# Two sums for the first norm, a new order of the third block pair, exchanged bank groups: one change in three places of a two-layer hybrid transformer kernel

## The chip, the cores and the metric

The kernel runs on one core of a Trainium2 chip. What is measured is the device time of one execution in microseconds (us). A profile is one further execution, taken by the hardware profiler.

## The reference, cut to what matters

Two layers work on 256 latent tokens and 256 context tokens of 1024 channels, all in float32. Each layer is a feed-forward block, a mixer (a short convolution in layer 0, grouped-query attention in layer 1) and a second feed-forward block. Each of the six norms is modulated by a vector that comes from the conditioning inputs:

```python
def _rms(t, g):
    y = t32 * lax.rsqrt(jnp.mean(t32 * t32, axis=-1, keepdims=True) + NORM_EPS)
    return y.astype(t.dtype) * g
def _modulate(t, g, shift, scale):
    return _rms(t, g) * (1 + scale) + shift
def _swiglu(h, w13, w2):
    gte, up = jnp.split(h @ w13, 2, axis=-1)
    return (jax.nn.silu(gte) * up) @ w2
...
mod = (jax.nn.silu(c) @ mod_w[i] + mod_b[i])          # 9 x 1024 per layer
lat = lat + 0.5 * mod[:, 0, 2] * _swiglu(_modulate(lat, norm_g[i, 0], mod[:, 0, 0], mod[:, 0, 1]), ...)
...                                                    # mixer, then a second _swiglu
y = ob.swapaxes(0, 1).reshape(bsz, t, D_MODEL) @ w_o   # attention, output projection
```

## The kernel before, in words

**Layout.** The state `x` lies with channels on the 128 partitions: eight blocks of 128 channels (k = 0 to 7), each 512 tokens wide (256 latent, 256 context). Every matrix product of two float32 operands is made of three TensorE products, because both operands are split into a high part (`hh`, `wh`; written by ScalarE) and a low part (`hl`, `wl`; written by VectorE as the rest): high by high, high by low, low by high. A helper `mm3` (lines 146 to 148) issues the three. Inside the first block the helper `part_of(i, k, n)` (line 1318) issues one of the three, n = 0 for `hh` by `wh`, 1 for `hh` by `wl`, 2 for `hl` by `wh`, for both halves `pg` and `pu` of output tile i: two TensorE instructions each time. `product(i, k)` is n = 0, 1, 2 for one k, `products(i, q)` is `product` for the block pair k = 2q, 2q + 1.

**The opening, written out by hand.** Inside `with tc.manual_schedule(engines=set(QUEUES))` the four queues TensorE, VectorE, ScalarE and SyncE issue in the order of the program text. The first block computes, while the weights still arrive, the mean of squares of every token, the modulation of the first norm and the first three output tiles (i = 0, 1, 2) of the first feed-forward product. Its steps are:

- `fill(idle, WARM)` (line 1080): 14 products of ones, which nobody reads, two TensorE instructions each.
- `spread_c` (line 1272): 16 steps that copy the activated conditioning over all partitions with a product by the identity `ident` (a part of the constants `cst`), two instructions each; `keep_c` (line 1278) moves the result out of the four `cs` banks.
- `square(k, ...)` writes the squares of block k (k = 0, 1 by VectorE, line 1149; the others by ScalarE, line 1151, k = 7 in two halves). `pair_sum(j)` (line 1155) adds two of them on VectorE, which leaves four partial sums; `token_sums(ps, k)` (line 1159) sums one over the partitions with 8 TensorE instructions, so 32 for the four.
- the root and reciprocal, `tile_rows` and `tile_turn` (lines 1171 and 1183; the modulation of one block by TensorE), the row products `rb` (line 1374), the normed block `over_tile` (line 1199), and `high_part` and `low_part` (lines 1290, 1298, 1303), which apply scale and shift and split into `hh` and `hl`.
- for the later blocks `mod_pe` and `mod_turn` (lines 1211 and 1233, then VectorE lines 1238 and 1245) give scale and shift of several blocks at once. Those of block 7 come from `end_units` (line 165, two units of VectorE for the scale and two for the shift), which read the tiles `mt`. `w_hi` and `w_lo` (lines 1135 and 1139) split the weights of the three output tiles in three pieces; `over_rms(q, ris)` (line 1283) norms a block pair; `norm_k` and `norm_q` are the high and low parts of one block or of a pair.

The end of the block is, before the change: three `products(i, 2)` for blocks 4 and 5 output tile by output tile, then block 6 for all three output tiles, then block 7 for all three.

**After it** the order is the planner's: outside of such blocks it orders the instructions by its own costs and by when operands come ready. There follow the gates of the three output tiles (`w13_post`: line 698 on ScalarE, line 700 on VectorE, the split at lines 122 and 123), the fourth and fifth output tile (`load_w` splits their weights at lines 122 and 123 into two halves of tags `wh`, `wl`, four buffers each, which the weights of the first two output tiles held; products at lines 146 to 148), and `FirstBlocks.sums` (lines 399 to 406), which builds sums of blocks for the rest of the product.

**The banks.** The accumulators lie in eight PSUM banks. `use_banks` opens groups of them in the order given, the first group on the lowest banks, and reuse is released tile by tile (`reuse_waits="tile"`). During attention the groups are `ptp` (banks 0, 1), `psc` (banks 2 to 5, tiles of two banks) and `pav` (banks 6, 7). The last `psc` tile is `py2`, the first two output tiles (m = 0, 1) of the output projection; it lies on banks 2 and 3. The projection's loop then reads it and exchanges the groups:

```python
    for m in range(KT):
        if m < 2:
            ps = py2[:, m, :]
        else:
            w = wo(m)
            ps = psum("py")
            for k in range(KT):
                mm3(ps[:, :S], w(k), aos[k], k == 0, k == KT - 1)
        gated(m, ps[:, :S], gate)          # VectorE, line 2007
        if m == 1:
            use_banks(("pss", 2), ("psm", 6))
```

`psum` takes the next of the six `psm` banks in turn, so m = 2 gets bank 2 before the change. The weights of m = 2, 3 are split at lines 1702 (ScalarE) and 1705 (VectorE).

Of the kernel before, what the change touches and what calls it, by code (L numbers as in the profile page):

```python
# [15 lines left out]
ALU = mybir.AluOpType  # L16
# [5 lines left out]
S = 256  # L22
T2 = 2 * S
# [6 lines left out]
EPS = 1e-6  # L30
FIRST = 5
PER_PAIR = 0.7
WARM = 14
HALVED = 2, 8
CUTS = (0, 256), (256, 512), (512, 1024)
CONSTS = (
# [12 lines left out]
def hybrid_kernel(ctx: ExitStack, tc: tile.TileContext, a: dict, out: bass.AP):  # L49
    nc = tc.nc  # L50
# [9 lines left out]
    def use_banks(*pools):  # L60
        stage.close()
        for name, bufs in pools:
            banks[name] = stage.enter_context(
                tc.tile_pool(
                    name=name, bufs=bufs, space=bass.MemoryType.PSUM, reuse_waits="tile"
                )
            )
# [351 lines left out]
    class Border:  # L419
# [38 lines left out]
        def square(self, i, s):  # L458
            sq = self.sq[i, s] = tp.tile([P, S], F32, name=nm("sq"), tag="t", bufs=3)
            nc.scalar.activation(out=sq, in_=x[:, 6 + i, s * S : s * S + S], func=AF.Square)  # L460
            self.scaled(6 + i, s)
# [615 lines left out]
    def fill(ps, n):  # L1077

        for _ in range(n):
            nc.tensor.matmul(ps[:, :P], square_ones, square_ones, start=True, stop=True)  # L1080
# [69 lines left out]
        else:  # L1150
            nc.scalar.activation(out=dst, in_=src, func=AF.Square)

    def pair_sum(j, c0=0, c1=T2):
        t = sqs[2 * j][:, c0:c1]
        nc.vector.tensor_tensor(out=t, in0=t, in1=sqs[2 * j + 1][:, c0:c1], op=ALU.add)

    def token_sums(ps, k):
        for i in range(4):
            nc.tensor.matmul(
                ps[:, i : i + 1], sqs[k][:, i * P : i * P + P], ones,  # L1160
                start=k == 0 and i == 0, stop=k == KT - 2, skip_group_check=True,
            )
# [92 lines left out]
    def end_units(ch):  # L1255
        for v in range(2):
            mod_unit(0, ch, KT - 1, end_raw[ch], v)
        if ch:
            nc.vector.scalar_tensor_tensor(
                out=A00[:, KT - 1, :], in0=modv[0, 1][:, KT - 1, :], scalar=1.0,  # L1260
                in1=normg[:, 0, 0, KT - 1 :].to_broadcast([P, 2]), op0=ALU.add, op1=ALU.mult,
            )
# [3 lines left out]
    def spread_c(i, n=1):  # L1266


        for i in range(i, i + n):
            v, k = i // KT, i % KT  # L1270
            o = k % 4 * P
            nc.tensor.matmul(
                spread[i // 4][:, o : o + P], sccol[:, k, v : v + 1].to_broadcast([P, P]), ident,
                start=True, stop=True,
            )
# [30 lines left out]
    def norm_k(k):  # L1306
        for s in range(2):
            high_part(k, s)
            low_part(k, s)

    def norm_q(q):
        for k in (2 * q, 2 * q + 1):
            norm_k(k)
# [10 lines left out]
    def product(i, k):  # L1324
        for n in range(3):
            part_of(i, k, n)

    def products(i, q):
        for k in (2 * q, 2 * q + 1):
            product(i, k)  # L1330
# [7 lines left out]
    with tc.manual_schedule(engines=set(QUEUES)):  # L1338
        for k in range(2):
            for ch in (1, 0):  # L1340
                ask_tile(ch, k)
            ask_w(k, 0)
        ask_w(2, 0)
        for ch in (1, 0):
            ask_mod(ch, 1)
        for i in range(2):
            ask_w(i, 1)
        table(AF.Silu)
        nc.scalar.activation(out=sccol[:, :, :2], in_=ccol, func=AF.Silu)
        table(AF.Sqrt)  # L1350
        for i in range(4):
            spread[i] = psum("cs")
        ps = psum("ss")
        fill(idle, WARM)
        spread_c(0, 6)
        for k, eng in enumerate((nc.vector, nc.vector) + (nc.scalar,) * 5):
            square(k, eng)
            if k % 2:
                pair_sum(k // 2)
                token_sums(ps, k - 1)  # L1360
                spread_c(6 + k // 2)
        for s in range(2):
            square(7, nc.scalar, s * S, s * S + S)
            pair_sum(3, s * S, s * S + S)
        token_sums(ps, 6)
        for i in range(2):
            keep_c(i)
        rs = tp.tile([P, 4], F32, name="rs4", tag="rs4", bufs=1)
        nc.scalar.activation(out=rs, in_=ps[:, :4], func=AF.Sqrt, scale=1.0 / D, bias=eps_t)
        nc.vector.reciprocal(rs, rs)  # L1370
        tile_rows(0)
        rb = psum("rb")
        for i in range(4):
            nc.tensor.matmul(
                rb[:, i * P : i * P + P], rs[:, i : i + 1].to_broadcast([P, P]), ident,
                start=True, stop=True,
            )
        nc.vector.tensor_scalar(
            out=sb1, in0=modb[:, 0, KT : 2 * KT], scalar1=1.0, scalar2=None, op0=ALU.add
        )  # L1380
        w_hi(0, 0)
        over_tile(0, 0, rb)
        tile_turn(0)
        over_tile(0, 1, rb)
        pps[0] = psum("pg"), psum("pu")
        spread_c(9, 7)
        for s in range(2):
            high_part(0, s)
        for i in range(2, 4):
            keep_c(i)  # L1390
        pps[1] = psum("pg"), psum("pu")
        w_lo(0, 0)
        for s in range(2):
            low_part(0, s)
        for s in range(2):
            part_of(0, 0, 0, s * S, s * S + S)
        part_of(0, 0, 1)
        tile_rows(1)
        for ch in (1, 0):
            ask_mod(ch, 2)  # L1400
        w_hi(1, 0)
        w_lo(1, 0)
        ris = tp.tile([P, T2], F32, name="ris", tag="gm", bufs=3)
        nc.scalar.copy(ris, rb)
        w_hi(2, 0)
        for s in range(2):
            over_tile(1, s, ris)
        part_of(0, 0, 2)
        part_of(1, 0, 0)
        tile_turn(1)  # L1410
        for n in (1, 2):
            part_of(1, 0, n)
        pps[2] = psum("pg"), psum("pu")
        part_of(2, 0, 0)
        w_lo(2, 0)
        for s in range(2):
            high_part(1, s)
            low_part(1, s)
        for n in (1, 2):
            part_of(2, 0, n)  # L1420
        product(0, 1)
        over_rms(1, ris)
        table(AF.Silu)
        mod_pe(1, 1)
        mod_pe(0, 1)
        for ch in (1, 0):
            ask_tile(ch, 2)
        ask_w(2, 1)
        for i, ch in enumerate((1, 0)):
            ask_end(ch)  # L1430
            ask_w(i, 2)
        ask_w(2, 2)
        product(1, 1)
        w_hi(0, 1)
        w_lo(0, 1)
        mod_turn(1, 1)
        mod_turn(0, 1)
        w_hi(1, 1)
        norm_q(1)
        product(2, 1)  # L1440
        products(0, 1)
        w_hi(2, 1)
        w_lo(1, 1)
        over_rms(2, ris)
        w_lo(2, 1)
        mod_pe(1, 2)
        mod_pe(0, 2)
        end_units(1)
        products(1, 1)
        w_hi(0, 2)  # L1450
        mod_turn(1, 2)
        mod_turn(0, 2)
        w_lo(0, 2)
        norm_q(2)
        products(2, 1)
        w_hi(1, 2)
        w_lo(1, 2)
        over_rms(3, ris)
        products(0, 2)
        w_hi(2, 2)  # L1460
        w_lo(2, 2)
        products(1, 2)
        norm_k(6)
        end_units(0)
        products(2, 2)
        for i in range(3):
            product(i, 6)
        norm_k(7)
        for i in range(3):
            product(i, 7)  # L1470
        for ch in HALVED:
            b = modb[:, :, ch * KT : ch * KT + KT]
            nc.vector.tensor_scalar(out=b, in0=b, scalar1=0.5, scalar2=None, op0=ALU.mult)
# [551 lines left out]
    for m in range(KT):  # L2025
        if m == KT - 2:
            ready()
# [6 lines that stand above are left out]
                mm3(ps[:, :S], w(k), aos[k], k == 0, k == KT - 1)  # L2034
        gated(m, ps[:, :S], gate)
        if m == 1:
            use_banks(("pss", 2), ("psm", 6))
        square_add(m, 0, S)
        hi, lo = xa(m, 0), xa(m, 1)
        nc.scalar.activation(out=hi[:, :S], in_=x[:, m, :S], func=AF.Identity, scale=A[:, m, :1])  # L2040
        nc.vector.scalar_tensor_tensor(
            out=lo[:, :S], in0=x[:, m, :S], scalar=A[:, m, :1], in1=hi[:, :S].bitcast(F32),
            op0=ALU.mult, op1=ALU.subtract,
        )
        for part, t in enumerate((hi, lo)):
            nc.scalar.copy(
                t[:, S:], bs[:, part, m : m + 1].bitcast(F32).to_broadcast([P, 2])
            )
# [260 lines left out]
```

## Time and profile before

| | |
|---|---|
| runs before | 1554.48 us median of 3 (1553.35 to 1557.8) |
| the profiled execution | 1553.15 us, of which the span of the instructions is 1551.4 us |
| granted TensorE clock, mean | 1.000 |
| TensorE busy | 1544.8 us of the span |
| VectorE busy | 1308.3 us |
| ScalarE busy | 763.7 us |
| data moved | 247.72 MB, 160 GB/s mean |

A row of the timeline gives the start in us from the start of the span, how long the row lasts in us, engine, line and operation, the written tile and the read ones (`out<-in`), the form, how many instructions are merged into the row (x28), and in brackets how long the engine was idle before it and what ended that. A TensorE row ends later than the next one starts, because products are pipelined: what one costs is the distance of the starts. A row of the windows gives for each engine the busy time and, in brackets, the number of instructions. DVE is VectorE, ACT ScalarE, PE TensorE, PEld its weight loads, SP SyncE.

### The profile page before, as it was taken

What the parts mean: (1) busy time and instruction counts of PE and PEld (TensorE: products, weight loads), DVE (VectorE), ACT (ScalarE), POOL (GpSimd) and SP (SyncE); (2) the same over time, 40 slices, a digit from 0 to 9 for tenths busy, and PEclk for the clock granted to TensorE, in tenths of its full rate; (3) what the DMA queues carried; (4) which work ended last, traced back from release to release, by engine and by line L of the source; (5) the groups of instructions that cost most, each with busy time, mean ns of one, the idle gap of its engine ahead of it and who ended that gap; (6) DMA issues with size and microseconds to landing.
All of it is one profiled execution on the core that took longest, in us unless ns stands there. A gap on an engine that the chain in (4) does not pass through costs nothing.

```text
span 1551.4 us, 25405 instructions
## 1 busy us (share of the span) xinstructions
PE 1544.8 (100%) x10296; PEld 1419.6 (92%) x10296; DVE 1308.3 (84%) x1944; ACT 763.7 (49%) x1285; POOL 28.9 (2%) x24
## 2 busy tenths in 40 slices
PE   9999999999999999999999999999999999999999
PEld 7899899989888899988999899988999899998888
DVE  5988889997999689987998989987998877878653
ACT  5554245536322475522554475522554465776551
POOL 0000000000000000000000000000000002220000
PEclk9999999999999999999999999999999999999999
DMA  9433633354565423355333632356344743346551
GB/s 358 136 109 129 211 123 123 121 201 167 178 221 195 140 86 119 114 178 197 123 129 124 218 120 105 114 189 227 136 142 165 264 146 120 109 171 244 190 176 70
DMA packets 52005, 247.72 MB, mean 160 GB/s; under 512 B 6064, under 2 KB 9264, under 8 KB 36656
## 3 DMA queue, kind: packets, MB, share of 16 engines
q1 hardware_dynamic: 51600, 245.91, 46.2%
q8 instruction: 80, 1.31, 0.3%
q14 instruction: 37, 0.30, 0.1%
q10 hardware_dynamic: 288, 0.19, 0.0%
HBM read 243.72 MB, written 1.05 MB: 158 GB/s over the span
## 4 chain that ended last, share of the span: by engine, by line
PE 99%; ACT 0%; DVE 0%; issue 0%; ACTq 0%
PE py L146 9%; PE py L148 9%; PE py L147 9%; PE p L146 7%; PE p L148 7%; PE p L147 7%; PE q L148 5%; PE q L146 5%; PE q L147 5%; PE py L1994 3%; PE pu L1994 3%; PE pg L1994 3%; PE pv L146 1%; PE pv L148 1%; PE pg L545 1%; PE pv L147 1%
## 5 line engine op out<-in xcount | busy, mean ns | idle before, releaser
L165 DVE CUSTOM_DVE_ANT_0 junk<-wm,scbc,cst 128x1024 bf16<-128x1024 f32 x224 | 287.2, 1282 | 32.3 <-DMA wm<-in_modT 30.6
L122 ACT ACTIVATE wh<-wr 128x1024 fp32r<-128x1024 f32 (+1 forms) x196 | 178.0, 925 | 215.8 <-PE py L147 124.9
L123 DVE TENSOR_TENSOR wl<-wr,wh 128x1024 fp32r<-128x1024 f32 (+1 forms) x196 | 205.8, 1060 | 51.5 <-PE py L1994 22.9
L146 PE MATMUL py<-gh,wh 128*128 128x512 f32 (+1 forms) x594 | 217.8, 367 | 0.0
L147 PE MATMUL py<-gl,wh 128*128 128x512 f32 (+1 forms) x594 | 217.3, 366 | 0.0
L148 PE MATMUL py<-gh,wl 128*128 128x512 f32 (+1 forms) x594 | 217.1, 365 | 0.0
L773 ACT ACTIVATE wh<-wr 128x1024 fp32r<-128x1024 f32 x165 | 169.5, 1056 | 86.1 <-DVE wr L796 65.5
L776 DVE TENSOR_TENSOR wl<-wr,wh 128x1024 fp32r<-128x1024 f32 x165 | 196.8, 1218 | 15.4 <-ACT wh L773 15.3
L148 PEld LDWEIGHTS py<-gh,wl 128*128 128x128 f32 x594 | 112.0, 189 | 17.9
L146 PEld LDWEIGHTS py<-gh,wh 128*128 128x128 f32 x594 | 112.1, 189 | 17.5
L147 PEld LDWEIGHTS py<-gl,wh 128*128 128x128 f32 x594 | 112.1, 189 | 17.4
L148 PE MATMUL p<-th,wl 128*128 128x256 f32 x440 | 124.5, 283 | 0.0
L147 PE MATMUL p<-tl,wh 128*128 128x256 f32 x440 | 124.5, 283 | 0.0
L146 PE MATMUL p<-th,wh 128*128 128x256 f32 x440 | 124.5, 283 | 0.0
L146 PE MATMUL q<-bh,wh 128*128 128x256 f32 x304 | 86.0, 283 | 0.0
L147 PE MATMUL q<-bl,wh 128*128 128x256 f32 x304 | 86.0, 283 | 0.0
L148 PE MATMUL q<-bh,wl 128*128 128x256 f32 x304 | 86.0, 283 | 0.0
L146 PEld LDWEIGHTS p<-th,wh 128*128 128x128 f32 x440 | 84.5, 192 | 0.2
L147 PEld LDWEIGHTS p<-tl,wh 128*128 128x128 f32 x440 | 84.5, 192 | 0.2
L148 PEld LDWEIGHTS p<-th,wl 128*128 128x128 f32 x440 | 84.5, 192 | 0.0
L791 DVE TENSOR_TENSOR wr<-wr 128x1024 f32<-128x1024 f32 x55 | 67.4, 1225 | 1.8
L148 PE MATMUL q<-th,wl 128*128 128x256 f32 x220 | 62.9, 286 | 0.0
(394 smaller groups left out, 4101.0 us busy)
## 6 DMA issues: line engine op xcount, KB each, us to landing
wr<-in_w SPq DMA_DIRECT2D x85, 1024.0 KB, 4.9
wm<-in_modT SPq DMA_DIRECT2D x128, 512.0 KB, 4.2
wr<-in_w2h SPq DMA_DIRECT2D x48, 704.0 KB, 4.4
wr<-in_cw_cx SPq DMA_DIRECT2D x8, 1024.0 KB, 5.6
wr<-in_w2l SPq DMA_DIRECT2D x8, 1024.0 KB, 4.9
mr<-in_mod SPq DMA_DIRECT2D x8, 512.0 KB, 8.6
wr<-in_cw_b SPq DMA_DIRECT2D x4, 1024.0 KB, 5.5
wr<-in_cw_out SPq DMA_DIRECT2D x4, 1024.0 KB, 5.2
```

Of the source, the lines that this page charges most:

```text
L122: nc.scalar.activation(out=hi, in_=src, func=AF.Copy)
L123: nc.vector.tensor_tensor(out=lo, in0=src, in1=hi.bitcast(F32), op=ALU.subtract)
L146: nc.tensor.matmul(ps, wh, mh, start=first, stop=False, **kw)
L147: nc.tensor.matmul(ps, wh, ml, start=False, stop=False, **kw)
L148: nc.tensor.matmul(ps, wl, mh, start=False, stop=last, **kw)
L165: nc.vector.tensor_tensor_reduce(out=junk, in0=raw, in1=scbc[:, v, :], scale=0.5 if ch in HALVED else 1.0, scalar=modb[:, l, col : col + 1 ...
L545: nc.tensor.matmul(ps, w[n == 1], hl if n == 2 else hh, start=first and n == 0 and k == ks[0] and (first is True or g == 0), stop=last and ...
L773: nc.scalar.activation(out=self.shaped(g, 0), in_=self.part(g), func=AF.Copy)
L776: nc.vector.tensor_tensor(out=self.shaped(g, 1), in0=self.part(g), in1=self.shaped(g, 0).bitcast(F32), op=ALU.subtract,)
L791: tt(out=by_two(raw[:, :1024]), in0=a21.unsqueeze(1).to_broadcast([P, 2, T2]), in1=by_two(raw)[:, :, :T2], op=ALU.subtract,)
L1994: nc.tensor.matmul(p[:, :n], w(j, k)[part], m(k)[:, :n], start=not part and k == 0, stop=part == 1 and k == nk - 1, skip_group_check=True,)
```

## The change

Three places are edited. In the opening, 11 and not 14 fills come first, all 16 steps of `spread_c` come at once instead of 6, then one behind each of three token sums, then 7 later, five more fills follow them, VectorE adds the squares of blocks 0 to 5 to one sum and those of 6 and 7 to another, and TensorE takes two `token_sums` instead of four; in the later place of the seven `spread_c` there are six fills. In the third block pair, the shift units of block 7 (`end_units(0)`) move up to directly behind its scale units, blocks 4 and 5 are multiplied in an order written out by part, blocks 6 and 7 are normed together, and their products run output tile by output tile. At the output projection the two bank groups are opened in the other order, so that `psm` starts at bank 0.

```diff
-WARM = 14
+WARM = 11
+FILL = 6
...
-    def pair_sum(j, c0=0, c1=T2):
-        t = sqs[2 * j][:, c0:c1]
-        nc.vector.tensor_tensor(out=t, in0=t, in1=sqs[2 * j + 1][:, c0:c1], op=ALU.add)
+    def add_square(i, k, c0=0, c1=T2):
+        t = sqs[i][:, c0:c1]
+        nc.vector.tensor_tensor(out=t, in0=t, in1=sqs[k][:, c0:c1], op=ALU.add)
...
         fill(idle, WARM)
-        spread_c(0, 6)
-        for k, eng in enumerate((nc.vector, nc.vector) + (nc.scalar,) * 5):
-            square(k, eng)
-            if k % 2:
-                pair_sum(k // 2)
-                token_sums(ps, k - 1)
-                spread_c(6 + k // 2)
-        for s in range(2):
-            square(7, nc.scalar, s * S, s * S + S)
-            pair_sum(3, s * S, s * S + S)
+        spread_c(0, 16)
+        fill(idle, 5)
+        for k in range(6):
+            square(k, nc.vector if k < 2 else nc.scalar)
+            if k:
+                add_square(0, k)
+        square(6, nc.scalar)
+        for c in (0, S):
+            square(7, nc.scalar, c, c + S)
+            add_square(6, 7, c, c + S)
+        token_sums(ps, 0)
         token_sums(ps, 6)
         for i in range(2):
             keep_c(i)
...
         over_tile(0, 1, rb)
         pps[0] = psum("pg"), psum("pu")
-        spread_c(9, 7)
+        fill(pps[0][0], FILL)
         for s in range(2):
             high_part(0, s)
...
         mod_pe(1, 2)
         mod_pe(0, 2)
         end_units(1)
+        end_units(0)
         products(1, 1)
         w_hi(0, 2)
         mod_turn(1, 2)
         mod_turn(0, 2)
         w_lo(0, 2)
         norm_q(2)
         products(2, 1)
         w_hi(1, 2)
         w_lo(1, 2)
         over_rms(3, ris)
-        products(0, 2)
         w_hi(2, 2)
         w_lo(2, 2)
-        products(1, 2)
-        norm_k(6)
-        end_units(0)
-        products(2, 2)
+        for i, k, n in (
+            (0, 4, 0), (0, 5, 0), (0, 4, 1), (0, 4, 2), (0, 5, 1),
+            (1, 4, 0), (1, 5, 0), (0, 5, 2), (1, 4, 2), (1, 5, 2), (1, 4, 1), (1, 5, 1),
+            (2, 4, 0), (2, 5, 0), (2, 4, 2), (2, 5, 2), (2, 4, 1), (2, 5, 1),
+        ):
+            part_of(i, k, n)
+        norm_q(3)
         for i in range(3):
-            product(i, 6)
-        norm_k(7)
-        for i in range(3):
-            product(i, 7)
+            products(i, 3)
...
         if m == 1:
-            use_banks(("pss", 2), ("psm", 6))
+            use_banks(("psm", 6), ("pss", 2))
```

## The prediction

> **What bounds the kernel now.** I read the page first (busy times, then the chain that ended last), then TensorE's waits, then the timeline of the places that the change touches.
>
> ```profile
> PE 1544.8 (100%) x10296; PEld 1419.6 (92%) x10296; DVE 1308.3 (84%) x1944; ACT 763.7 (49%) x1285; POOL 28.9 (2%) x24
> ...
> PE 99%; ACT 0%; DVE 0%; issue 0%; ACTq 0%
> ```
>
> ```profile
> PE py L146 <- DVE x L2007: 1.3, 1, 1.3
> PE idle L1080 <- DVE eps_t L105: 1.1, 1, 1.1
> PE pg L146 <- ACT wh L122: 0.7, 1, 0.7
> ```
>
> TensorE is busy throughout, its own instructions make 99% of the chain, and it has three waits in the whole run: the start, one of 0.7 us ahead of the fourth output tile's `pg`, one of 1.3 us in the output projection. So work taken from VectorE or ScalarE is worth nothing unless it ends one of these waits, and the whole change can gain little more than the two waits plus whatever it takes from TensorE's own list. What it can lose is larger: every stall that a new order makes on TensorE is added in full.
>
> **Part one, the opening.** Here TensorE's timeline, then the landing of the constants, then ScalarE and VectorE beside it.
>
> ```profile
> 1.07 6.29 PE L1080 MATMUL idle<-sones 128*128 128x128 f32 x28 [1.07 <-DVE eps_t L105]
> 7.19 1.50 PE L1272 MATMUL cs<-cst,sccol 128*128 128x128 f32 x12
> 8.53 0.95 PE L1159 MATMUL ss<-ones,sq 128*128 128x1 f32 x8
> 9.34 0.47 PE L1272 MATMUL cs<-cst,sccol 128*128 128x128 f32 x2
> ...
> 11.88 0.95 PE L1159 MATMUL ss<-ones,sq 128*128 128x1 f32 x8
> ...
> 17.02 0.28 PE L1318 MATMUL pg<-hh,wh 128*128 128x256 f32 x1
> ```
>
> ```profile
> L89 ACTq DMA_DIRECT2D cst<-in_cst x1: 450/450/450, 1.2 to 1.2; - x1
> ...
> DMA to landing us min/median/max: 5.4/5.4/5.4
> ```
>
> ```profile
> 6.52 2.29 ACT L1151 ACTIVATE sq<-x 128x512 f32<-128x512 f32 x4
> ...
> 15.76 1.09 ACT L1290 ACTIVATE hh<-hr,mod,A 128x256 fp32r<-128x256 f32 x2 [0.86 <-DVE mod L1191]
> ```
>
> ```profile
> 7.69 0.69 DVE L1155 TENSOR_TENSOR sq<-sq,sq 128x512 f32<-128x512 f32 x1 [1.01 <-ACT sq L1151]
> ...
> 10.01 0.76 DVE L1155 TENSOR_TENSOR sq<-sq,sq 128x256 f32<-128x256 f32 x2 [0.47 <-ACT sq L1151]
> ```
>
> The two more additions of VectorE cost nothing: the five go into one sum, the last four behind ScalarE's squares, which are ready from about 7.1 on (four in 2.29 us from 6.52). Four times 0.69 from 7.1 ends at 9.9, before the last pair at 10.01, which ends at 10.77 as before. TensorE reads that sum after 11.88 already now, so the cover is over 1 us, and the additions would cost only what they overran it.
>
> Nor do the sums bind TensorE, so only its own list counts. Ahead of `tile_rows` it held 28 instructions of fills, 18 of spreading and 32 of token sums, 78 in all; now it holds 22, 32, 10 more fills and 16 token sums, 80. Sixteen instructions go and eighteen come. But the rows show two paces: the 28 fills take 6.12 us (1.07 to 7.19), 0.219 each, the 12 of the spreading take 1.34 us (7.19 to 8.53), 0.112 each, in the same shape. The slow pace is that of the first 6 us, not of an instruction. In that time the kernel before does 28 instructions. The new list has only 22 that can run: the 23rd reads the constants, which land at 1.16 + 5.4 = 6.6 (the row prints the start as 1.2). 22 fills end at 1.07 + 22 x 0.219 = 5.9, so TensorE stands for 0.7 us, does 2.7 instructions until 7.19, the other 29.3 of the spreading at 0.112 until 10.5, ten fills until 11.6, and two token sums of 0.81 us each (8.53 to 9.34) until 13.2. Before, the fourth ends at 11.88 + 0.81 = 12.7. That is 0.5 us later, and all the rest of the chain (root, reciprocal, row products, high parts) hangs on it.
>
> Later, 12 instructions of fills stand in for 14 of spreading, at most 2 x 0.112 = 0.22 us less. The second high part ends at 15.76 + 1.09 = 16.85 and TensorE takes it at 17.02, so of the 0.22 only about 0.1 can be used before that high part is what is late. The opening costs 0.4 us. Its bounds: -0.1, if the constants arrive before 5.9 (then the token sums end at 12.8, and the 0.22 may count in full), and +3.2, if the pause prolongs the slow pace (rival one).
>
> **Part two, the third block pair.** TensorE first, then VectorE, then ScalarE.
>
> ```profile
> 43.41 0.39 PE L1318 MATMUL pg<-hh,wh 128*128 128x512 f32 x1
> ...
> 59.51 0.39 PE L1318 MATMUL pu<-hl,wh 128*128 128x512 f32 x1
> 60.59 0.50 PE L146 MATMUL pg<-hh,wh 128*128 128x512 f32 x1 [0.70 <-ACT wh L122]
> ```
>
> ```profile
> 35.45 1.28 DVE L165 CUSTOM_DVE_ANT_0 junk<-mt,scbc,cst 128x1024 bf16<-128x1024 f32 x1
> ...
> 38.10 0.16 DVE L1259 SCALAR_TENSOR_TENSOR A<-mod,cst 128x2 f32<-128x2 f32 x1
> 40.13 0.17 DVE L1238 TENSOR_TENSOR A<-pr,sb 128x6 f32<-128x6 f32 x1 [1.87 <-PE pr L1233]
> ...
> 40.80 0.17 DVE L1238 TENSOR_TENSOR mod<-pr,cst 128x6 f32<-128x6 f32 x1 [0.31 <-PE pr L1233]
> ...
> 42.11 0.41 DVE L1298 TENSOR_SCALAR hr<-hr,A,mod 128x256 f32<-128x256 f32 x1
> ...
> 45.26 1.28 DVE L1139 TENSOR_TENSOR wl<-wr,wh 128x512 fp32r<-128x512 f32 x2
> ...
> 48.87 0.41 DVE L1298 TENSOR_SCALAR hr<-hr,A,mod 128x256 f32<-128x256 f32 x1
> ```
>
> ```profile
> 41.00 2.08 ACT L1290 ACTIVATE hh<-hr,mod,A 128x256 fp32r<-128x256 f32 x4 [2.83 <-DVE mod L1238]
> ...
> 57.54 1.05 ACT L122 ACTIVATE wh<-wr 128x1024 fp32r<-128x1024 f32 x1
> ...
> 59.49 1.05 ACT L122 ACTIVATE wh<-wr 128x1024 fp32r<-128x1024 f32 x1
> ```
>
> TensorE does the same 72 instructions, one per 0.227 us ((59.51 - 43.41) / 71), without a stall. The end is what changes. The weights of the fourth output tile take the buffers of the first, and these come free when output tile 0 is done: after 60 instructions before, at 43.41 + 13.6 = 57.0 (ScalarE starts `wh` at 57.54), after 48 now, at 54.3. Its two high halves, which end at 60.54, can be ready 2.7 us earlier, at 57.8. TensorE wants them at 59.74. The wait goes: 60.59 - 59.51 - 0.23 = 0.85 us gained.
>
> The moved shift units are two of VectorE, 2.65 us (35.45 to 38.10, a scale pair); they issue no DMA. They go where VectorE idled 1.87 us, and what is queued behind them is the scale and shift of blocks 4 to 6: the row of 40.13 moves to 40.9, that of 40.80 to 41.3, so ScalarE's four high parts end at 43.6 instead of 43.1. TensorE's new order wants the high parts of block 5 at its second step, 43.41 + 0.45 = 43.86: cover 0.3 us, the thinnest of the change. The others have more. Low parts of block 5, which end with the row before 45.26, come at 45.8 and are wanted at the eighth step, 46.6. The low weights of output tile 1 come at 47.0 and are wanted at 47.9. Blocks 6 and 7, with the units gone from between them, have four low parts of 0.79 (42.11 to 45.26) from 49.4 to 52.5; their last is wanted at 51.6 + 2.3 = 53.8. If the cover of 0.3 us fails, the price is what it is overrun by, at most some 0.5 us. The later opening moves all of these alike. Part two: -0.85, bounds -1.0 (with the slow restart behind the wait) and -0.3.
>
> **Part three, the banks.**
>
> ```profile
> 1343.04 0.28 PE L147 MATMUL py<-a,wh 128*128 128x256 f32 x1
> 1343.16 0.28 PE L148 MATMUL py<-a,wl 128*128 128x256 f32 x1
> 1344.74 0.39 PE L146 MATMUL py<-a,wh 128*128 128x256 f32 x1 [1.31 <-DVE x L2007]
> ```
>
> ```profile
> 1342.68 1.22 DVE L1705 TENSOR_TENSOR wl<-wr,wh 128x1024 fp32r<-128x1024 f32 x1 [0.52 <-ACT wh L1702]
> 1343.82 0.87 DVE L2007 SCALAR_TENSOR_TENSOR x<-py,mod,x 128x256 f32<-128x256 f32 x2
> ```
>
> ```profile
> 1295.55 0.40 PE L146 MATMUL psc<-kh,qh 128*128 128x512 f32 x1
> ...
> 1295.81 0.60 ACT L1595 ACTIVATE sq<-pq 128x512 f32<-128x512 f32 x1
> ```
>
> Output tile 2 waits for both rows of line 2007, because it gets the bank of `py2`, which they read. With `psm` from bank 0 it gets a bank of `ptp`, whose readers are long through. That a new group doesn't wait for all of the old ones shows at 1295.55: there TensorE writes a tile of a new group, while ScalarE reads `pq` of the old group only at 1295.81. So the wait goes: 1344.74 - 1343.16 - 0.12 = 1.46 us. Next late are the low weights for k = 4 to 7, ready at 1343.90 and wanted at 1343.28 + 14 x 0.12 = 1344.96. The `py2` banks now come to output tile 4, 48 products later, when line 2007 has been through for over 4 us. Bounds: -1.6 (with the slow restart) and -0.4, if those weights bind after all.
>
> **The sum** is +0.4 - 0.85 - 1.46 = -1.9 us. The profiled execution took 1553.15 us, its span 1551.4, so 1.75 lie around the span and are not touched. The median of the runs is 1554.48; I set the sum against the middle of the two, 1553.8, which gives 1551.9.
>
> **The rivals.** One: *the pause keeps the slow pace.* TensorE's pace halves its time per instruction at 7.19, 6.12 us after its first one, without a pause in between; in the new list there is one of 0.7 us just ahead of that. If it made the 6.12 us start anew at 6.6, only 28 of the 58 remaining instructions would be done by 12.7 and the rest would end at 16.0, 2.8 us after my 13.2. I take half, 1.4: the sum becomes -0.5, the time 1553.3. For it: the change of pace comes late after the start. Against it: the pause is short beside the fills around it, and nothing in this trace shows a pause there. [...]
>
> Two, slower: *VectorE's queue behind the block is planned worse.*
>
> ```profile
> 60.00:70.00 10.00, 9.41 (x41) 7.80 (x42) 10.00 (x17) 8.00 (x13) 0.00 (x0) 1.00 0.32 107
> ```
>
> ```profile
> 67.87 2.49 DVE L123 TENSOR_TENSOR tl<-hr,th 128x512 fp32r<-128x512 f32 x4
> 70.28 2.35 DVE L123 TENSOR_TENSOR wl<-wr,wh 128x1024 fp32r<-128x1024 f32 x2
> ```
>
> From here VectorE has no idle time and the planner chooses its order anew, because the gates come earlier. If it puts the sixteen instructions of the block sums (0.62 each, 9.9 us) ahead of the fourth output tile's two low halves (1.18 each), these end at 52.5 + 9.9 + 2.4 = 64.8, where TensorE in plain order wants them at about 60.4: a stall of 4.4 us, a sum of +2.5, the time 1556.3. It decides from the point where the stall exceeds 1.9 us, that is, where the second low half ends after 62.3. Against it: VectorE comes to this place 2 us earlier than before, and TensorE stalled nowhere between this block and the projection.
>
> Three: *the exchange does not do what it says*, because the group is released as a whole; then the projection keeps its wait, the sum is -0.4, the time 1553.4. The row at 1295.55 speaks against it.
>
> **How the numbers follow.** Forecast 0.55, late pace 0.2, planner 0.12, banks 0.05, and 0.08 for a gain that I don't see. About 0.3%, 4.7 us, is what a measurement of this kernel can tell from no change. The forecast, the late pace and the banks lie within it; the planner's case passes it where more than this one place is planned worse; a gain beyond it needs twice what the waits hold, or scatter of the runs. Hence 0.18 faster, 0.7 within, 0.12 slower. The range goes from 1549.0 (the best bounds, -0.1 - 1.0 - 1.6 = -2.7, and the 1.1 by which the lowest run lies under the median, and a little more) to 1557.0, which takes in rivals one to three.
>
> **What would show it.** Right: `cs` rows start at 6.6 behind 22 fills and a pause, the last token sum ends at about 13.2, the fourth output tile's `pg` follows the last line 1318 without a wait, and output tile 2 starts 0.12 us after `py2`'s last product. Wrong: a slow pace past 7.2 us, a wait of TensorE for `hh` near 44, for `wl` near 61, or any new row among its waits.

## The result, and the profile after

| | median, us | lowest to highest, runs | profiled execution, us |
|---|---|---|---|
| before, in this comparison | 1557.55 | 1553.15 to 1558.8, 14 | 1553.15 (span 1551.4) |
| after | 1551.76 | 1551.17 to 1553.34, 14 | 1552.99 (span 1551.2) |

The ratio of after to before is 0.9971, with a 95% interval from 0.9963 to 0.9979: 0.29% faster (the means of the runs, 1556.51 and 1551.98 us, give it; the two medians lie further apart, 0.9963). That is the predicted time, but not the predicted difference: 1.9 of 1553.8 us is 0.12%, outside the interval. The times of the kernel before lie in groups on every chip: 4 of its 14 here from 1553.15 to 1554.48, the others from 1556.2 to 1558.8. The execution that was profiled for the prediction, 1553.15 us, was of the lowest group. After the change, 10 of 14 lie from 1551.17 to 1551.90 and 4 from 1552.99 to 1553.34, and the profiled execution is one of the upper. The spans of the instructions separate them as clearly: 1549.3 to 1549.7 us for the ten, 1551.1 to 1551.4 for the four. So the two profiles that one would naturally lay side by side differ by 0.16 us, the medians by 5.8.

TensorE's list of waits in the kernel after (us in total, times, longest):

```profile
PE idle L1081 <- DVE eps_t L106: 1.1, 1, 1.1
PE cs L1273 <- DMA cst<-in_cst: 0.6, 1, 0.6
```

Both waits that the change aimed at are gone (0.7 us for `wh`, 1.3 us for `x`), and there is one new one of 0.6 us, for the constants. Lines from the opening on have moved down by one or two in the kernel after: 1273 is `spread_c`, 1160 the token sums, 1319 `part_of`, 147 to 149 are `mm3`. TensorE's timeline of the profile after, at the three places:

```profile
1.07 5.06 PE L1081 MATMUL idle<-sones 128*128 128x128 f32 x22 [1.07 <-DVE eps_t L106]
6.71 5.54 PE L1273 MATMUL cs<-cst,sccol 128*128 128x128 f32 x32 [0.58 <-DMA cst<-in_cst]
12.10 1.28 PE L1081 MATMUL idle<-sones 128*128 128x128 f32 x10
13.21 1.84 PE L1160 MATMUL ss<-ones,sq 128*128 128x1 f32 x16
14.99 1.08 PE L1172 MATMUL pr<-mr,sccol 128*32 128x128 f32 x32
...
61.70 0.39 PE L1319 MATMUL pu<-hl,wh 128*128 128x512 f32 x1
61.93 0.39 PE L147 MATMUL pg<-hh,wh 128*128 128x512 f32 x1
...
1344.41 0.28 PE L149 MATMUL py<-a,wl 128*128 128x256 f32 x1
1344.53 0.28 PE L147 MATMUL py<-a,wh 128*128 128x256 f32 x1
```

At the second place the fourth output tile follows 0.23 us behind the last product of the block, at the third output tile 2 follows 0.12 us behind the last product of `py2`: no wait at either. In the opening the 22 fills end before the constants are there, as predicted, but then the 32 instructions of `spread_c` take 5.39 us (6.71 to 12.10). At the fast pace they would take 32 x 0.112 = 3.58. So some 17 of them went at the slow pace of the start, (5.39 - 3.58) / (0.219 - 0.112), and the clock came up only at 6.71 + 17 x 0.219, about 10.4 us. The granted clock of the profile (PEclk) can't show this: it reads 1.00 in this stretch too, as it does ahead of 7.19 us in the profile before, so a late first rise is read from the pace of the rows alone. This is rival one, in the execution that happened to be profiled.

### The profile page after: what moved, and what is told of

Read it like the earlier page. It is cut to its first block, busy times and chain, and to the rows that moved or that the text cites. A ratio compares the mean times of both kernels' runs of the same rounds, so it can differ in the third digit from the quotient of the medians.

```text
span 1551.2 us, 25416 instructions
## 1 busy us (share of the span) xinstructions
PE 1546.1 (100%) x10296; PEld 1420.9 (92%) x10296; DVE 1309.5 (84%) x1946; ACT 762.7 (49%) x1285; POOL 28.9 (2%) x24
## 3 DMA queue, kind: packets, MB, share of 16 engines
q8 instruction: 80, 1.31, 0.3%
## 4 chain that ended last, share of the span: by engine, by line
PE 99%; DMA 0%; ACT 0%; DVE 0%; ACTq 0%; issue 0%
PE py L147 9%; PE py L148 9%; PE py L149 9%; PE p L147 7%; PE p L149 7%; PE p L148 7%; PE q L149 5%; PE q L147 5%; PE q L148 5%; PE py L1996 3%; PE pu L1996 3%; PE pg L1996 3%; PE pg L1319 1%; PE pv L149 1%; PE pv L147 1%; PE pg L546 1%
```

## The experiments

The theory after the result: in most of its executions the kernel before loses some 3 us to a TensorE clock that falls back to half during the opening (a granted clock of 0.50 in b_again's windows below), and the new opening prevents that; parts two and three are worth what was predicted. The rival: the times of before lie apart for a reason outside the opening, and the three parts bring the gain by shorter lists and fewer waits alone. The kernels are each part alone, the suspected causes alone, and both kernels unchanged again. All ratios are to the kernel before on the same chip, with the 95% interval.

| kernel | median | lowest to highest, runs | ratio |
|---|---|---|---|
| b_again | 1554.97 | 1552.98 to 1558.96, 11 | 0.9997 (0.9987 to 1.0008) |
| only_opening | 1553.95 | 1553.60 to 1555.24, 11 | 0.9990 (0.9981 to 0.9999) |
| only_third | 1553.83 | 1552.08 to 1556.99, 11 | 0.9992 (0.9982 to 1.0002) |
| only_banks | 1554.60 | 1551.48 to 1556.39, 11 | 0.9990 (0.9980 to 1.0000) |
| a_four | 1554.88 | 1553.07 to 1556.26, 11 | 0.9997 (0.9987 to 1.0006) |
| a_no5 | 1550.31 | 1550.25 to 1552.25, 5 | 0.9967 (0.9955 to 0.9980) |
| a_fill0 | 1551.72 | 1551.19 to 1554.52, 11 | 0.9977 (0.9969 to 0.9986) |
| a_w14 | 1551.31 | 1551.20 to 1551.59, 7 | 0.9971 (0.9960 to 0.9982) |
| b_two | 1555.64 | 1554.17 to 1556.31, 12 | 0.9999 (0.9990 to 1.0007) |
| a_w14_no5 | 1550.37 | 1550.34 to 1550.48, 5 | 0.9967 (0.9955 to 0.9979) |
| a_again | 1551.46 | 1551.26 to 1552.22, 8 | 0.9974 (0.9964 to 0.9984) |

### b_again: the kernel before, unchanged

> The kernel before, unchanged. Its 14 times lie in two groups, four at 1553.2 to 1554.5 and ten at 1556.2 to 1558.8 us; the profile shown is of the lower group. Theory one, the start: in the upper group TensorE stays at, or falls back to, the slow pace of 0.219 us per 128x128 instruction later than 7.19 us, in the opening with its 32 small token sums. Then a profile of an execution near 1557.5 shows rows of the opening later by 4 us before 20 us and the same waits of 0.7 and 1.3 us after. Theory two, the waits: the opening is the same, and a wait of TensorE behind 40 us is 4 us longer. Theory three, the memory: the loss is spread over the whole run with no one place. All three expect a ratio of 1.000 to itself within 0.002.

Its profiled execution took 1556.45 us, one of an upper group. TensorE's timeline of it, then the windows with the granted clock, which is the column behind the engines (PEclk):

```profile
11.62 1.19 PE L1159 MATMUL ss<-ones,sq 128*128 128x1 f32 x8
12.73 1.93 PE L1171 MATMUL pr<-mr,sccol 128*32 128x128 f32 x32
14.60 2.08 PE L1374 MATMUL rb<-cst,rs 128*128 128x128 f32 x8
...
19.61 0.36 PE L1318 MATMUL pg<-hh,wh 128*128 128x256 f32 x1
```

```profile
11.00:12.00 1.00, 1.00 (x12) 1.00 (x11) 0.00 (x0) 0.28 (x1) 0.00 (x0) 1.00 1.08 363
12.00:13.00 1.00, 1.00 (x14) 0.96 (x17) 0.00 (x0) 0.16 (x1) 0.00 (x0) 0.59 1.01 406
...
18.00:19.00 1.00, 1.00 (x6) 1.00 (x6) 1.00 (x4) 1.00 (x3) 0.00 (x0) 0.50 1.05 422
19.00:20.00 1.00, 1.00 (x11) 1.00 (x10) 0.93 (x4) 0.54 (x2) 0.00 (x0) 1.00 1.01 401
```

Here is what the profile of before in the prediction could not show. The clock is full at 11 to 12, falls to a half within 12 to 13 (0.59 is 0.18 us at full speed and the rest at half, so at 12.2) and is full again from 19: 6.8 us at half, although TensorE is busy for the whole of each of these windows. The rows of that time take almost twice as long: `tile_rows` moves on after 1.87 us (12.73 to 14.60), where it took 1.0 in the undisturbed execution. The two executions are level up to there (`tile_rows` starts at 12.73 here, at 12.76 in the first profile of before):

```profile
12.76 1.08 PE L1171 MATMUL pr<-mr,sccol 128*32 128x128 f32 x32
13.77 1.16 PE L1374 MATMUL rb<-cst,rs 128*128 128x128 f32 x8
...
16.70 0.36 PE L1318 MATMUL pg<-hh,wh 128*128 128x256 f32 x1
```

The first `pg` product comes 2.9 us later, 19.61 against 16.70; the whole execution is 3.3 us longer, 1556.45 against 1553.15.

For the executions that weren't profiled, the record has the span of the instructions and the mean granted clock. Of the kernel before, 76 executions on three chips were taken beside the experiments:

| mean granted clock | executions | span, us |
|---|---|---|
| 1.000 | 17 | 1551.1 to 1551.6 |
| 0.999 | 19 | 1552.3 to 1553.6 |
| 0.998 | 28 | 1554.2 to 1554.9 |
| 0.997 or 0.996 | 12 | 1555.6 to 1556.1 |

Each step down goes with a span some 1.5 us longer, so the groups are the clock, in 59 of 76 executions. The 6.8 us at half of b_again take 0.5 x 6.8 / 1551 = 0.0022 off the mean, which is its 0.998; by the same working 0.999 is about 3.1 us at half (0.001 x 1551 / 0.5) and 0.997 about 9.3 (an estimate from means that are rounded to three places). The place is not in these numbers; the next kernel shows it.

### only_opening: part one alone

The first part of the diff in the kernel before; the third block pair and the banks as before.

> Part one alone: fills, spreading, two sums instead of four. Theory one (the upper group of the kernel before is a late pace of its start, and the new opening ends it): no time above 1556; times at 1553.6 (1553.15 + 0.4) and 1555.3 (with the pace released one step later), ratio about 0.998. Theory two or three (the upper group has nothing to do with the opening): the two groups stay, at 1553.6 and 1558.0, ratio 1.0003.

```profile
13.17 1.08 PE L1172 MATMUL pr<-mr,sccol 128*32 128x128 f32 x32
```

Its lowest time is 0.62 us above b_again's lowest (1553.60 against 1552.98), and `tile_rows` starts 0.41 us later than in the undisturbed kernel before (13.17 against 12.76). So the list does cost about what the prediction said; the second `tile_rows` is 0.39 us later too (18.21 against 17.82). But the granted clock is 1.000 in all 11 executions, where the kernel before has that in 9 of 33 on the same chip, and the spans all lie from 1551.7 to 1552.2 us. (The times up to 1555.24 come from what lies around the span, 1.8 to 3.1 us.) Only the opening was changed, so it is the opening that decides whether the clock falls, and there b_again's profile has the fall. Over the runs the part is a gain, 0.1%: the part that was predicted to cost is no cost, because it keeps the clock from falling.

### only_third and only_banks: parts two and three alone

> Part two alone: the order of the third block pair. By the working of the prediction the wait of 0.7 us ahead of the fourth output tile goes and 0.85 to 1.0 us are gained: groups at 1552.3 and 1556.6, ratio 0.9994. Theory two (the upper group is a longer wait here): only the lower group is left, ratio 0.998. Theory one: both groups stay.

> Part three alone: the bank groups exchanged. By the working of the prediction the wait of 1.3 us in the output projection goes and 1.46 to 1.6 us are gained: groups at 1551.7 and 1556.1, ratio 0.9990. If the group were released as a whole, the wait would stay and the ratio be 1.0000. Theory one: both groups stay.

The lowest times lie 0.90 us (1552.08) and 1.50 us (1551.48) under b_again's lowest, against 0.85 and 1.46 predicted. Their lists of waits, only_third first, only_banks second:

```profile
PE py L146 <- DVE x L2007: 1.3, 1, 1.3
PE idle L1080 <- DVE eps_t L105: 1.1, 1, 1.1
```

```profile
PE idle L1080 <- DVE eps_t L105: 1.1, 1, 1.1
PE pg L146 <- ACT wh L122: 0.7, 1, 0.7
PE cs L1272 <- DMA cst<-in_cst: 0.6, 1, 0.6
```

Each lacks just the wait that its part was to remove. The third row of only_banks belongs to the old opening: in this execution the 28 fills took 5.32 us instead of 6.29, since the clock came up earlier, and then TensorE stood for the constants (b_again has a pause of 0.4 us there). Both keep the old opening and its spread of times, up to 1556.99 and 1556.39, with a granted clock of 1.000 in only 3 of 11 each; the profiled execution of only_banks, 1554.74 us, has `tile_rows` at the slow pace again:

```profile
13.13 1.93 PE L1171 MATMUL pr<-mr,sccol 128*32 128x128 f32 x32
```

The three parts alone give -0.10, -0.08 and -0.10%, together -0.28%; the whole gave -0.29%. The parts add up, within intervals of about 0.1% each.

### a_four: four token sums in the kernel after

```diff
-            if k:
-                add_square(0, k)
+            if k % 2:
+                add_square(k - 1, k)
...
-        token_sums(ps, 0)
-        token_sums(ps, 6)
+        for k in (0, 2, 4, 6):
+            token_sums(ps, k)
```

> The changed kernel with four partial sums again and four token sums (32 one-column instructions of TensorE) in one row behind the five fills; all else of the change stays. [...] Then 16 more of them (3.5 us in a row) bring the fall back: times above 1554.5 appear, and even without it the list is 1.6 us longer (ratio about 0.999 or 1.000). Theory B, the spreading: what ended the fall is that the 16 spreading steps and the fills stand in a block ahead of the sums; then there is no fall and the times lie at 1552.8 and 1554.6, ratio 0.998.

```profile
11.64 3.63 PE L1160 MATMUL ss<-ones,sq 128*128 128x1 f32 x32
15.20 1.08 PE L1172 MATMUL pr<-mr,sccol 128*32 128x128 f32 x32
```

The sixteen more instructions cost what they hold where the clock stays up: 3.56 us for 32 is 0.11 each, `tile_rows` starts at 15.20, and the profiled execution takes 1553.19 us. But 9 of the 11 times lie from 1554.55 to 1556.26, and the whole gain of the change is gone (0.9997). Times above 1554.5 are what theory A has, that it is the number of one-column instructions that counts; theory B has none above 1554.6 and a ratio of 0.998. With four token sums, 3.6 us in which each instruction has a single moving column, the spread of the kernel before is back: the granted clock is 0.999 or 0.998 in these nine executions and 1.000 in the two lowest. Where it fell in them was not profiled.

### b_two: two sums, the spreading left as it was

The kernel before, with VectorE's additions to two sums and two `token_sums`, but 14 fills first, nine steps of `spread_c` at once and seven later, and no further fills.

> The kernel before with the two sums alone: squares added to two sums, two token sums instead of four; the first nine spreading steps ahead of them, the seven later ones and the 14 fills where they were, no further fills. Its list is 16 instructions shorter; the sums end at about 11.7 instead of 12.7 us, with a pause of some 0.7 us while VectorE adds. Theory A (the number of one-column instructions alone decides whether the pace falls): no fall, times at 1552.0 to 1553.5, ratio 0.9975. [...]

```profile
10.20 2.43 PE L1159 MATMUL ss<-ones,sq 128*128 128x1 f32 x16 [1.31 <-DVE sq L1155]
12.56 1.93 PE L1171 MATMUL pr<-mr,sccol 128*32 128x128 f32 x32
```

```profile
12.00:18.00 6.00, 6.00 (x52) 5.50 (x52) 1.41 (x7) 1.63 (x5) 0.00 (x0) 0.50 1.05 402
```

Fewer token sums are not enough. Here they come early, TensorE waits 1.31 us for the sum, and the clock is at a half for the whole of 12 to 18. None of 12 times is under 1554.17, and the granted clock is 0.999 or 0.998 in all 12. So it isn't the number of one-column instructions by itself: with half of them and a wait ahead of them the clock falls too. In the kernel after, all of `spread_c` and the five fills stand where this kernel waits. That what counts is how poor a stretch is in full-width products (theory C, also below) fits both kernels, but how poor, and for how long, was not measured.

### a_no5, a_fill0, a_w14: the fills

`a_no5` leaves out `fill(idle, 5)`, `a_fill0` leaves out `fill(pps[0][0], FILL)`, `a_w14` has `WARM = 14` and not 11; the rest is the kernel after.

> The changed kernel without the five fills ahead of the token sums: ten TensorE instructions of 0.112 us fewer on a list that binds. If the five fills are not needed to hold the clock (theory A: two token sums are too short to make it fall): 1.1 us less, times at 1550.1 and 1551.9, ratio 0.9965. [...]

> The changed kernel without the six later fills, those on the first pg bank. TensorE then stands until the high part of block 0 is ready. By the timeline that high part is late by 0.1 us already with the fills, so without theory C it gains 0.0 to 0.1 us and the ratio stays at 0.997. By theory C the stretch with tile rows and row products and no fills lets the pace fall in part of the executions: some 2 to 4 us higher times, ratio 0.998 or more.

> The changed kernel with 14 instead of 11 fills at the start, so that TensorE stands less ahead of the spreading while the constants land. In the changed kernel's profile the fast pace came only at 10.36 us, with a pause of 0.58 us in the stretch before 6.95; its times are ten at 1551.2 to 1551.9 and four at 1553.0 to 1553.3. If the pause is the cause of the upper four: no time above 1552.5, the rest 0 to 0.5 us higher than 1551.2 (in the executions in which the slow pace lasts past 6.6 us the six more instructions cost up to 0.4 us). If it is not: four in fourteen stay at 1553.

TensorE without the five fills:

```profile
10.29 1.94 PE L1160 MATMUL ss<-ones,sq 128*128 128x1 f32 x16
12.16 1.08 PE L1172 MATMUL pr<-mr,sccol 128*32 128x128 f32 x32
```

`tile_rows` starts 1.17 us earlier than in a_again (13.33, quoted below), and the time falls by 1.15 (1550.31 against 1551.46; a_again ran on another chip, and a_w14, on the same one, has 1551.31). The granted clock is 1.000 in all five executions, so the five fills were not needed here, where all 16 steps of `spread_c` stand ahead of the sums; five executions are few.

The six fills in the later place are another matter. TensorE's timeline without them, and the windows:

```profile
16.81 0.39 PE L1319 MATMUL pg<-hh,wh 128*128 128x256 f32 x1 [1.14 <-ACT hh L1291]
...
18.20 1.67 PE L1172 MATMUL pr<-mr,sccol 128*32 128x128 f32 x32
```

```profile
18.00:19.00 1.00, 1.00 (x24) 0.81 (x26) 0.66 (x2) 0.21 (x1) 0.00 (x0) 0.77 1.05 422
19.00:21.00 2.00, 2.00 (x20) 1.25 (x12) 0.37 (x2) 1.09 (x4) 0.00 (x0) 0.50 1.01 395
21.00:22.00 1.00, 1.00 (x6) 0.90 (x4) 0.98 (x4) 1.00 (x3) 0.00 (x0) 0.53 1.10 365
```

They stand in a wait of 1.14 us for the first high part, so they cost next to nothing; without them the clock falls 1.7 us after that wait in this execution. The median stays (1551.72), the highest time is 1554.52, and the granted clock is 0.999 in 4 of 11 executions, where the kernel after has 1.000 in all 22 (14 in the result, 8 in a_again).

With three more fills at the start the pause ahead of the constants does not go away in the profile of a_w14:

```profile
6.77 3.81 PE L1273 MATMUL cs<-cst,sccol 128*128 128x128 f32 x32 [0.62 <-DMA cst<-in_cst]
```

But in this execution the clock was up ahead of the pause: the 28 fills took 5.08 us, where the slow pace takes 6.32 (a_w14_no5 below). None of 7 times is above 1551.59. In the kernel after, 4 of 14 were at 1553 and above, in a_again 0 of 8, and in only_opening, by the spans, 0 of 11. That fits the pause as the cause of the late clock, but so few runs don't show it.

### a_w14_no5 and a_again: the version that the experiments point to

```diff
-WARM = 11
+WARM = 14
...
         spread_c(0, 16)
-        fill(idle, 5)
```

> The changed kernel with 14 fills at the start and without the five ahead of the sums. If the pause among the first fills makes the upper group near 1552.3 to 1553 and the five fills are not needed: no upper group, all times at 1550.1 to 1550.6, ratio 0.996. If the five fills are needed in some phases of the clock: part of the times at 1552 or above.

> The changed kernel again, on the same chip as the two others. Times at 1551.2 to 1551.9 and about a quarter near 1553; ratio 0.997. A profile of the lower group should show the fast pace by 6.95 us at the latest and the last token sum ending near 13.2, by the sum of the prediction; of the upper group, near 15.0.

TensorE's timeline of a_w14_no5, then of a_again, which is the kernel after in an execution whose clock came up in time. The profile puts the wait of 1.10 us down to ScalarE's `table`; by the program `spread_c` reads only the activated conditioning and the constants, and in the profile of the kernel after the constants land at about that time, at 1.15 + 5.4 = 6.6 us.

```profile
1.07 6.32 PE L1081 MATMUL idle<-sones 128*128 128x128 f32 x28 [1.07 <-DVE eps_t L106]
7.20 3.75 PE L1273 MATMUL cs<-cst,sccol 128*128 128x128 f32 x32
```

```profile
1.07 4.63 PE L1081 MATMUL idle<-sones 128*128 128x128 f32 x22 [1.07 <-DVE eps_t L106]
6.80 3.81 PE L1273 MATMUL cs<-cst,sccol 128*128 128x128 f32 x32 [1.10 <-ACT table L1086]
10.44 1.28 PE L1081 MATMUL idle<-sones 128*128 128x128 f32 x10
11.56 1.84 PE L1160 MATMUL ss<-ones,sq 128*128 128x1 f32 x16
13.33 1.08 PE L1172 MATMUL pr<-mr,sccol 128*32 128x128 f32 x32
...
60.35 0.39 PE L147 MATMUL pg<-hh,wh 128*128 128x512 f32 x1
...
1342.98 0.28 PE L147 MATMUL py<-a,wh 128*128 128x256 f32 x1
```

The clock of a_again came up at about 5.0 us (its 22 fills took 4.63 us, where the slow pace takes 5.06); the 6.95 of two of the expectations was their author's estimate, and no run shows that moment. In a_w14_no5 the fills reach the constants even at the slow pace (28 of them, to 7.20), and there is no pause. Its five times lie within 0.14 us, and its median is 1.09 us under that of a_again on the same chip (1550.37 against 1551.46). It is better than both kernels: 0.9967 (0.9955 to 0.9979) of before. Against the kernel after the gain is shown by the times, which do not overlap; a_no5, with the shorter start, has the same median and one of five times at 1552.25.

## Why the prediction was right or wrong, point by point

**Against an execution whose clock stays up, the steps hold.** a_again beside the first profile of before, by the starts of the same instructions: `tile_rows` is 0.57 us later (13.33 against 12.76), the fourth output tile's `pg` 0.24 us earlier (60.35 against 60.59), output tile 2 of the projection 1.76 us earlier (1342.98 against 1344.74). Each less the one before it gives the terms: opening +0.57, third pair -0.81, banks -1.52. Predicted were +0.4, -0.85 and -1.46. The parts alone gave +0.6, -0.9 and -1.5 by their lowest times. The spans differ by 1.7 us (1549.7 against 1551.4), predicted 1.9. Parts two and three are right in mechanism and size. That the opening's size fits is in part chance: in a_again the clock came up not at 7.2 us, as the working has it, but at about 5.0, ahead of the pause (its 22 fills took 4.63 us and not 5.06), and the spreading started at 6.80 and not at 6.6.

**The step that failed is the opening's, "the opening costs 0.4 us", and its bounds of -0.1 to +3.2.** It was worked out from one execution, in which the clock came up at 7.2 us and stayed up. That holds only for those executions of before whose clock stays up, 17 of the 76 on record. Of the others, the profiled one (b_again) loses 2.9 us in this very place to a clock that falls to a half, and only_banks and b_two, which have fewer wide products ahead of the sums than the new opening, show the half pace there too. The new opening keeps clear of that: the granted clock is 1.000 in all 33 executions of it (14 after, 8 a_again, 11 only_opening). Over the runs the term is a gain: 0.1% of 1554 us is 1.6 us (0.2 to 3.0 by the interval). The bound below, -0.1, was reasoned from the instructions of the list; that the same list could run at another pace in other executions was seen only where it would hurt the change (rival one), not where it hurt the kernel before.

**The base failed with it.** The sum was set against 1553.8, between the profiled execution and the median of three. In the comparison the kernel before had a median of 1557.55. The predicted time, 1551.9, came within 0.2 us because base and forecast were both near the times of executions whose clock stays up. That these are the rule after the change is the work of the opening, for which the prediction had only a cost; so the hit is luck in that respect.

**Rival one came about, and in the profile itself.** Two of the prediction's own signs of being wrong are there: a slow pace past 7.2 us, and a new row among the waits. The pause, 0.58 us, was where it was predicted, and the clock came up 3.2 us later than in the first profile of before (10.4 against 7.2). `tile_rows` starts at 14.99 in place of 13.33: 1.66 us. The prediction took 1.4, half of the 2.8 for the whole of a new start, and that half was its author's estimate. Of the two profiled executions of the kernel after, one has the loss and the other, a_again, does not. It does not come each time: 4 of 14 in the result, none of 8 later. The chance of 0.2 was meant for the outcome of the comparison; that it is near this share of the executions is chance.

**The other rivals did not.** The planner put no new wait behind the block: TensorE's list after has no row behind the opening. The exchange of the groups does what it says (rival three): output tile 2 follows at 0.12 us. The thinnest cover, 0.3 us ahead of block 5's high parts, held: no row among the waits names `hh`, in either profile of the kernel after.

**What is left open.** Of the executions of the kernel before, two were profiled (1553.15 and 1556.45). That the other groups are the clock too is shown by their granted clock, and that the cause is in the opening by only_opening; at which moment it falls in them was not seen. How full of wide products a stretch must be to hold the clock wasn't measured, and that a pause delays the first rise rests on one profile.

## What to carry to other kernels

Before a sum is made against a profiled execution, look where its time lies among the runs: if the times lie in groups, the profile is of one group, and the gain may lie in how often the others occur. A stretch of TensorE at the start of a kernel is to be judged by what holds the clock as well as by its own instructions: a late first rise of the clock behind a pause cost 1.7 us here, a fall behind a row of one-column products 3.3, more than any instruction in it, and the fills that stand in a wait anyway were next to free (medians of 1551.76 and 1551.46 with them, 1551.72 without). The mean granted clock of each execution, where it is on record, told such falls apart without a profile (1.000 in 17 of 76 executions, 0.999 to 0.996 in 59); the late first rise showed in the span alone (1551.1 to 1551.4 us in 4 of 14, 1549.3 to 1549.7 in 10, all at 1.000). When a change aims at waits, list the waits of before and after; here two rows gone were 2.3 us predicted and 2.4 measured (by the lowest times).

## What the runs showed of the hardware that was not expected

The granted clock fell while TensorE was shown busy. In b_again it went to 0.50 at 12.2 us, with TensorE busy for 1.00 us in each of the windows shown. What lies ahead of that is token sums of 8 products with one moving column each (the last group from 11.62 to 12.73), then products onto 32 columns. The half pace lasted 6.8 us in b_again and from 18.5 to 21.9, 3.4 us, in a_fill0 (worked out as above from 0.77 in the window 18 to 19 and 0.53 in that of 21 to 22).

The changes of the clock lay at like distances in the four profiles that show a fall. The first rise is worked out from the row of the fills: at the slow pace 28 take 6.32 us (a_w14_no5) and 22 take 5.06 (after), and each fill at the fast pace takes 0.107 us off that; the fall and the return from the granted clock of the windows, as above.

| run | fills | first rise, us | granted clock at the fall | fall, us | granted clock at the return | return, us |
|---|---|---|---|---|---|---|
| b_again | 28 in 5.42 us | 5.4 | 0.59 in 12 to 13 | 12.2 | 0.50 in 18 to 19, 1.00 in 19 to 20 | 19.0 |
| only_banks | 28 in 5.32 us | 5.2 | 0.98 in 11 to 12 | 12.0 | 0.60 in 18 to 19 | 18.8 |
| b_two | 28 in 5.09 us | 4.7 | 0.74 in 11 to 12 | 11.5 | 0.84 in 18 to 19 | 18.3 |
| a_fill0 | 22 in 4.53 us | 4.8 | 0.77 in 18 to 19 | 18.5 | 0.53 in 21 to 22 | 21.9 |

In the first three the clock fell 6.8 us after the first rise and stayed at half for 6.8; in a_fill0 it fell 13.7 us after and stayed for 3.4. The 6.8 is twice the 3.4 and the 13.7 four times it, to 0.1 us.

With the old opening the clock first came up at 7.2 us in the profile before and 7.0 us in only_third, which stayed at full, and at 5.4 us in b_again and 5.2 us in only_banks, which fell. So whether the row of token sums costs anything goes with the moment of the first rise, which differs from one execution of a kernel to the next; four profiles don't make that a rule.

A short pause can go with a late first rise, but not by its length alone. The 0.58 us of waiting ahead of the constants in the profile after went with a clock that came up at 10.4 us. Pauses of 0.50 us in only_opening and 0.75 us in a_four, at the same place and behind 22 fills that were all slow too (5.06 us), went with one that was up for all of `spread_c`. Their rows, only_opening first:

```profile
6.63 3.81 PE L1273 MATMUL cs<-cst,sccol 128*128 128x128 f32 x32 [0.50 <-ACT table L1086]
```

```profile
6.88 3.81 PE L1273 MATMUL cs<-cst,sccol 128*128 128x128 f32 x32 [0.75 <-ACT table L1086]
```

The pause of 1.10 us in a_again says nothing on this, since the clock was up ahead of it. Which of the two occurs is a matter of the execution; what decides it was not measured.
